# Opening of a two-layer decoder trunk: first weights from a second DMA queue in smaller pieces, and nine products of a cleared tile on TensorE ahead of the work

## Chip, cores and metric

One core of one Trainium2 chip. The time is device microseconds of one execution of the whole program; lower is better. All numbers of the trace are from one profiled execution of the kernel before.

## What is computed

The reference is a trunk of two layers over 256 tokens of 1024 channels in float32. Each layer adds half a SwiGLU, then a mixer (an S5 state space in the first, sparse attention in the second), then half a SwiGLU again. The change lies ahead of the first SwiGLU:

```python
def _rmsnorm(x, g):
    y = x * lax.rsqrt(jnp.mean(x * x, axis=-1, keepdims=True) + RMS_EPS)
    return y * g

def _swiglu(x, w_in, w_out):          # w_in: 1024 x 5632, w_out: 2816 x 1024
    a, b = jnp.split(x @ w_in, 2, axis=-1)
    return (jax.nn.silu(a) * b) @ w_out

h = h + 0.5 * _swiglu(_rmsnorm(h, ffn1_norm[0]), ffn1_w_in[0], ffn1_w_out[0])
```

## The kernel before

The 256 tokens are two token tiles of 128 rows, `h[:, 0]` and `h[:, 1]`. To multiply, the kernel needs h transposed: `Acts.fill(t, kq)` (L152) turns four 128 x 128 blocks on TensorE (L156) into a PSUM bank `tr` and splits them into a high and a low part, `xT`: ScalarE writes the rounded high part (L140), VectorE the difference (L141). Weights come in granules of 1 MB, `raw`, [128, 2048], that is four slabs of 512 columns; `rawp` holds two. `split_half` (L78) makes a high part `whi` (ScalarE, L96 with the gain of the norm, L86 without) and a low part `wlo` (VectorE, L99 or L92), for which there are five buffers of two slabs each. Every product is three matmuls (`mm3`, L112): high by high (L115), high by low (L116), low by high (L117).

The feed-forward block (`ffn`, L177) goes over 11 chunks c of 256 hidden channels. A chunk takes eight slabs of w_in (two granules) into two PSUM banks `mm`, one for each token tile; ScalarE and VectorE make g = silu(a) * b from them (L235, L236), which frees the banks. In the next chunk TensorE turns g (L190), ScalarE and VectorE split it into `gT` (L140, L141), and `second` (L200) multiplies it by one granule of w_out into four banks `o`, 24 matmuls. Chunk 0 takes token tile 0 first in groups of four slabs (`gemm`, `lead=True`), so that it can begin before tile 1 is there.

A granule's DMA is issued on SP (`load_granule`, L68) and waits until VectorE has done the last split of the granule that had the buffer. In the first block `background` queues steps of `s5_prepare` (L251) between the slabs: small VectorE operations on [128, 32] (names s_...), products on GpSimd and VectorE for the tables Cw, cosT, sinT. Each engine works its instructions strictly in the order that the scheduler of the framework has written; that order follows from the code and from the scheduler's own estimate of times.

The opening (L53 to L76) issues, all on SP: the identity, tile 0 of x, the gains, the first half of the first granule (`raw0`), tile 1 of x, the second half of `raw0`. Meanwhile ScalarE loads its table (L59). The next granules and the constants of S5 follow on SP.

Of the kernel before, what the change touches and what calls it, by code (L numbers as in the profile page):

```python
# [9 lines left out]
F32 = mybir.dt.float32  # L10
# [6 lines left out]
P = 128  # L17
# [15 lines left out]
def kernel(ctx: ExitStack, tc: tile.TileContext, A, out):  # L33
# [19 lines left out]
    # ---- constants and gains  # L53
# [3 lines left out]
    nhalf = pers.tile([P, 8], F32, name="nhalf")  # L57
    V.memset(nhalf, -0.5)
    S.activation(small.tile([P, 8], F32, name="warm"), nhalf, AF.Silu)  # L59
    nc.sync.dma_start(out=ident, in_=A["ident"])  # L60
    nc.sync.dma_start(out=h[:, 0, :], in_=A["x"][0])
    nc.sync.dma_start(out=gains, in_=A["gains"])

    # ---- weights: each granule is split exactly into hi + lo parts as it arrives, scaled by the gain of its rows
# [8 lines left out]
    raw0 = rawp.tile([P, 2048], F32, name="raw")  # L73
    nc.sync.dma_start(out=raw0[:, 0:1024], in_=A["w_in1_0"][0, 0][:, 0:1024])
# [3 lines left out]
    def split_half(raw, j, w, gain, k0, eng="av"):  # L78
        """eng: which engines round and subtract"""
# [39 lines left out]
    def gemm(acc, xT, gen, kts=KT, lead=False):  # L119
        """acc[t] = x[t] @ W over kts slabs; lead: token tile 0 goes first in groups of four slabs"""  # L120
# [8 lines left out]
    # ---- 1/rms of the rows of one token tile of h, from its two halves  # L129
# [14 lines left out]
    # ---- h^T as hi and lo parts, channels on partitions, with 1/rms of its rows  # L144
# [21 lines left out]
    def background(bg, n):  # L166
        """n steps of other work, queued behind what has been issued so far"""
# [8 lines left out]
    # ---- res += 1/2 SwiGLU(rmsnorm(h)); done(t, half) once a half of token tile t of res is complete  # L176
    def ffn(x, gi, w_in, w_out, res, perm=False, bg=None, steps=1, done=None, first=()):  # L177
        with tc.tile_pool(name="ffn", bufs=2) as fp, tc.tile_pool(name="ps_a", bufs=1, space=PSUM) as pa:
# [5 lines left out]
            def transposed(g):  # L184
                """g^T of one chunk, hi and lo, tokens in natural order"""
# [58 lines left out]
    # ---- S5 in chunks of four tokens: discretisation, rotation tables, and stationary operands  # L244
# [6 lines left out]
    def s5_prepare(kp, sp, W):  # L251
# [36 lines left out]
        def exp_parts(x):  # L288
            """2^n and exp(r) - 1 with x = n ln2 + r."""
# [53 lines left out]
        def products(x, y, t4_):  # L343
            """x_re y_re, x_im y_im, x_re y_im, x_im y_re"""
            for t_, i, j in zip(t4_, (0, 1, 0, 1), (0, 1, 1, 0)):
                tt(t_, x[i], b16(y[j]), ALU.mult, G)
# [118 lines left out]
    # ---- h += S5(rmsnorm(h)); token 4 c + 2 t + e is in row 64 e + c of token tile t  # L465
# [21 lines left out]
    def s5(hc, x, W, kp, done):  # L487
        cosT, sinT, Cw, Wi, WBT, r4 = W.cosT, W.sinT, W.Cw, W.Wi, W.WBT, W.r4
        with tc.tile_pool(name="s5r", bufs=1) as rp, tc.tile_pool(name="s5w", bufs=2) as wp, \
# [16 lines left out]
            def u_transposed(b0, nb):  # L506
                """u^T of 2 nb groups of 32 channels"""
# [13 lines left out]
            def rotated(cb):  # L521
                """the tables of four groups, for the real and the imaginary half"""
# [104 lines left out]
    # ---- shared keys and values  # L627
# [489 lines left out]
```

## Time and profile before

| | us |
|---|---|
| median of three runs | 1074.84 |
| lowest and highest run | 1074.09, 1077.22 |
| span of the profiled execution, first to last instruction | 1070.4 |
| TensorE busy in that span | 1002.3 |
| VectorE busy | 708.6 |
| ScalarE busy | 574.7 |

The profile shows the span, and the profiled execution has no other time of its own; the median of the runs is 4.4 us above it, which is what lies around the span. Matmuls are pipelined and their ends are modelled, so that the lengths of two neighbours overlap; the distance of their starts is what one of them costs. In a row of the timeline stand the start, the length, the engine, the line, the operation with out<-in, the shapes, and in brackets the idle time of the engine just ahead with what ended it. Names are those of the program without buffer numbers.

### The profile page before, as it was taken

What the parts mean: (1) busy time and instruction counts of PE and PEld (TensorE: products, weight loads), DVE (VectorE), ACT (ScalarE), POOL (GpSimd) and SP (SyncE); (2) the same over time, 40 slices, a digit from 0 to 9 for tenths busy, and PEclk for the clock granted to TensorE, in tenths of its full rate; (3) what the DMA queues carried; (4) which work ended last, traced back from release to release, by engine and by line L of the source; (5) the groups of instructions that cost most, each with busy time, mean ns of one, the idle gap of its engine ahead of it and who ended that gap; (6) DMA issues with size and microseconds to landing.
All of it is one profiled execution on the core that took longest, in us unless ns stands there. A gap on an engine that the chain in (4) does not pass through costs nothing.

```text
span 1070.4 us, 14818 instructions
## 1 busy us (share of the span) xinstructions
PE 1002.3 (94%) x5553; PEld 807.9 (75%) x5553; DVE 708.6 (66%) x1403; ACT 574.7 (54%) x1051; POOL 180.5 (17%) x185
## 2 busy tenths in 40 slices
PE   7978999988879899999999999999977899999998
PEld 6766877876657688887887888887866678888886
DVE  5999755949875465656757555655688866656553
ACT  6443566643335464655665555554786656545451
POOL 6375100305732000000005100000203220000000
PEclk9988999999989999999999999999988999999999
DMA  6553544420328865555464455554303146555551
GB/s 237 183 187 118 197 158 140 163 91 24 137 103 205 331 201 193 197 176 181 170 221 158 158 187 173 191 197 145 100 1 118 40 138 214 170 186 197 185 176 72
DMA packets 27912, 171.74 MB, mean 160 GB/s; under 512 B 4544, under 2 KB 4992, under 8 KB 9024
## 3 DMA queue, kind: packets, MB, share of 16 engines
q1 hardware_dynamic: 26192, 164.77, 44.5%
q0 software_dynamic: 1648, 6.03, 2.2%
q8 instruction: 43, 0.70, 0.3%
q14 instruction: 29, 0.24, 0.1%
HBM read 165.54 MB, written 5.24 MB: 160 GB/s over the span
## 4 chain that ended last, share of the span: by engine, by line
PE 73%; DVE 14%; DMA 4%; ACT 4%; POOL 3%; issue 2%; SPq 0%; ACTq 0%; POOLq 0%; DVEq 0%
PE mm L115 14%; PE mm L116 13%; PE mm L117 13%; PE o L117 7%; PE o L115 7%; PE o L116 7%; DMA raw<-in_w_in_dram 4%; DVE wlo L99 4%; DVE wlo L92 2%; PE tr L190 1%; DVE w L544 1%; ACT whi L96 1%; DVE Pt L906 1%; ACT Pt L895 1%; PE tr L913 1%
## 5 line engine op out<-in xcount | busy, mean ns | idle before, releaser
L99 DVE SCALAR_TENSOR_TENSOR wlo<-raw,gains,whi 128x512 fp32r<-128x512 f32 (+2 forms) x408 | 295.7, 759 | 130.6 <-ACT whi L96 126.7
L96 ACT ACTIVATE whi<-raw,gains 128x512 fp32r<-128x512 f32 (+2 forms) x408 | 267.3, 699 | 187.2 <-PE mm L117 60.8
L115 PE MATMUL mm<-whi,xT 128*128 128x512 f32 (+2 forms) x800 | 313.5, 392 | 4.5 <-ACT whi L96 3.5
L117 PE MATMUL mm<-whi,xT 128*128 128x512 f32 (+2 forms) x800 | 307.1, 384 | 0.0
L116 PE MATMUL mm<-wlo,xT 128*128 128x512 f32 (+2 forms) x800 | 306.8, 384 | 0.3 <-DVE wlo L99 0.3
L92 DVE TENSOR_TENSOR wlo<-raw,whi 128x512 fp32r<-128x512 f32 x192 | 135.0, 743 | 95.3 <-ACT whi L86 95.1
L86 ACT ACTIVATE whi<-raw 128x1024 fp32r<-128x1024 f32 x104 | 108.8, 1057 | 133.6 <-PE mm L117 62.1
L115 PEld LDWEIGHTS mm<-whi,xT 128*128 128x128 f32 x800 | 151.1, 189 | 36.0 <-ACT whi L96 4.8
L117 PEld LDWEIGHTS mm<-whi,xT 128*128 128x128 f32 x800 | 150.9, 189 | 29.8
L116 PEld LDWEIGHTS mm<-wlo,xT 128*128 128x128 f32 x800 | 151.2, 189 | 28.4 <-DVE wlo L99 1.1
L115 PE MATMUL o<-whi,gT 128*128 128x512 f32 x352 | 143.0, 406 | 9.5 <-ACT gT L140 9.5
L117 PE MATMUL o<-whi,gT 128*128 128x512 f32 x352 | 141.6, 404 | 8.1 <-DVE gT L141 7.9
L116 PE MATMUL o<-wlo,gT 128*128 128x512 f32 x352 | 141.4, 402 | 0.0
L115 PEld LDWEIGHTS o<-whi,gT 128*128 128x128 f32 x352 | 67.7, 192 | 27.5 <-ACT gT L140 11.9
L117 PEld LDWEIGHTS o<-whi,gT 128*128 128x128 f32 x352 | 67.6, 192 | 26.3 <-DVE gT L141 10.1
L116 PEld LDWEIGHTS o<-wlo,gT 128*128 128x128 f32 x352 | 67.7, 192 | 15.7
L235 ACT ACTIVATE g<-mm,rs 128x256 f32<-128x256 f32 x88 | 40.7, 471 | 27.7 <-PE mm L117 27.6
L236 DVE SCALAR_TENSOR_TENSOR g<-mm,rs,g 128x256 f32<-128x256 f32 x88 | 41.9, 483 | 19.9 <-ACT g L235 19.4
L141 DVE TENSOR_TENSOR gT<-tr,gT 128x512 fp32r<-128x512 f32 (+1 forms) x55 | 36.4, 661 | 25.9 <-ACT gT L140 25.6
L140 ACT ACTIVATE gT<-tr 128x512 fp32r<-128x512 f32 (+1 forms) x55 | 33.3, 605 | 33.4 <-PE tr L190 26.7
L137 POOL TENSOR_TENSOR rs<-ms,nhalf 128x1 f32<-128x1 f32 x12 | 7.2, 600 | 231.7 <-DVE ms L136 231.6
L895 ACT ACTIVATE Pt<-Pt,mx 128x128 f32<-128x128 f32 (+1 forms) x64 | 28.4, 445 | 6.4 <-DVE mx L890 6.3
(311 smaller groups left out, 1009.1 us busy)
## 6 DMA issues: line engine op xcount, KB each, us to landing
raw<-in_w_in_dram SPq DMA_DIRECT2D x87, 1024.0 KB, 4.9
raw<-in_w_out_dram SPq DMA_DIRECT2D x44, 1024.0 KB, 4.9
raw<-in_w_kv_dram SPq DMA_DIRECT2D x6, 1024.0 KB, 4.8
raw<-in_w_glu_dram SPq DMA_DIRECT2D x4, 1024.0 KB, 4.8
raw<-in_w_o_dram SPq DMA_DIRECT2D x4, 1024.0 KB, 4.9
revd<-rev POOLq DMA_DIRECT2D x8, 384.0 KB, 15.0
raw<-in_w_qg_dram SPq DMA_DIRECT2D x6, 512.0 KB, 3.6
B<-revd POOLq DMA_DIRECT2D x1, 2048.0 KB, 13.2
```

The source lines that it names most:

```text
L86: Last.act = S.activation(hi, r, AF.Copy)
L92: i = el.tensor_tensor(out=lo[:, c], in0=r[:, c], in1=hi[:, c].bitcast(F32), op=ALU.subtract)
L96: Last.act = S.activation(hi[:, c], r[:, c], AF.Identity, scale=g_)
L99: i = V.scalar_tensor_tensor(out=lo[:, c], in0=r[:, c], scalar=g_, in1=hi[:, c].bitcast(F32), op0=ALU.mult, op1=ALU.subtract)
L115: T.matmul(ps, lhsT=xh, rhs=wh, start=start, stop=False)
L116: T.matmul(ps, lhsT=xh, rhs=wl, start=False, stop=False)
L117: Last.pe = T.matmul(ps, lhsT=xl, rhs=wh, start=False, stop=stop_)
L140: i = S.activation(dst_hi, src, AF.Copy)
L141: V.tensor_tensor(out=dst_lo, in0=src, in1=dst_hi.bitcast(F32), op=ALU.subtract)
L235: Last.act = S.activation(sl, acc[t][:, 0:256], AF.Silu, scale=rs[:, t:t + 1])
L236: Last.dve = V.scalar_tensor_tensor(out=g[:, t, :], in0=acc[t][:, 256:512], scalar=rs[:, t:t + 1], in1=sl, op0=ALU.mult, op1=ALU.mult)
L895: S.activation(Pt[:, r, br], Pt[:, r, br], AF.Exp, scale=-1.0, bias=mx[:, c:c + 1], accum_out=sm[:, c:c + 1])
```

## The change

It does four things. The first half of `raw0` is issued on ScalarE's DMA queue in two pieces of 256 KB, ahead of ScalarE's table load. Tile 0 of x is issued on SP in two halves, and the identity and the gains come between them instead of ahead of the whole and behind it. VectorE clears a tile `blank` of 128 x 128, and TensorE multiplies it by itself nine times into a `tr` bank that nothing reads. Since these calls shift the estimate of the scheduler, it writes a different order on all engines for the first five chunks of the first feed-forward block; behind them the orders are the same.

```diff
+    raw0 = rawp.tile([P, 2048], F32, name="raw")
+    nc.scalar.dma_start(out=raw0[:, 0:512], in_=A["w_in1_0"][0, 0][:, 0:512])
+    nc.scalar.dma_start(out=raw0[:, 512:1024], in_=A["w_in1_0"][0, 0][:, 512:1024])
+    blank = small.tile([P, P], F32, name="blank", bufs=1)
+    V.memset(blank, 0.0)
     V.memset(nhalf, -0.5)
+    for i in range(2):
+        nc.sync.dma_start(out=h[:, 0, i * 512:(i + 1) * 512], in_=A["x"][0][:, i * 512:(i + 1) * 512])
+        if i == 0:
+            nc.sync.dma_start(out=ident, in_=A["ident"])
+            nc.sync.dma_start(out=gains, in_=A["gains"])
     S.activation(small.tile([P, 8], F32, name="warm"), nhalf, AF.Silu)
-    nc.sync.dma_start(out=ident, in_=A["ident"])
-    nc.sync.dma_start(out=h[:, 0, :], in_=A["x"][0])
-    nc.sync.dma_start(out=gains, in_=A["gains"])
...
-    raw0 = rawp.tile([P, 2048], F32, name="raw")
-    nc.sync.dma_start(out=raw0[:, 0:1024], in_=A["w_in1_0"][0, 0][:, 0:1024])
     nc.sync.dma_start(out=h[:, 1, :], in_=A["x"][1])
     nc.sync.dma_start(out=raw0[:, 1024:2048], in_=A["w_in1_0"][0, 0][:, 1024:2048])
...
                 x = Acts(h)
+                run = tr_bank()
+                for _ in range(9):
+                    T.matmul(run[:, 0:P], lhsT=blank, rhs=blank, start=True, stop=True)
                 for t in range(2):
                     for hf in range(2):
                         x.fill(t, hf)
```

In the changed file the same lines stand five further down (L96 is L101, L99 is L104, L140 and L141 are L145 and L146, L236 is L241, L260 is L265).

First place: ScalarE at the start of the program. xT is the high part of the transposed tiles, whi that of a slab, junk the squares for the norm. Before:

```order
L59 ACT_TABLE_LOAD
L59 ACTIVATE warm<-nhalf 128x8
L140 ACTIVATE xT<-tr 128x4x128
L96 ACTIVATE whi<-raw,gains 128x512
L140 ACTIVATE xT<-tr 128x4x128
L96 ACTIVATE whi<-raw,gains 128x512
L140 ACTIVATE xT<-tr 128x4x128 x2
L132 ACTIVATE junk,ss<-h 128x512
L96 ACTIVATE whi<-raw,gains 128x512
```

And now:

```order
L59 DMA raw<-in_w_in_0_dram 128x512
L60 DMA raw<-in_w_in_0_dram 128x512
L69 ACT_TABLE_LOAD
L69 ACTIVATE warm<-nhalf 128x8
L101 ACTIVATE whi<-raw,gains 128x512 x2
L145 ACTIVATE xT<-tr 128x4x128 x3
L101 ACTIVATE whi<-raw,gains 128x512
L145 ACTIVATE xT<-tr 128x4x128
L137 ACTIVATE junk,ss<-h 128x512
```

Two DMA issues have come to the front, and both splits of the first half granule now stand ahead of tile 0's xT. A little further on, chunk 1's first four splits stand ahead of chunk 0's g, where it was two before.

Second place: VectorE at the last four splits of chunk 2 (the granule ahead of which s_tr and behind which the w_out granule stands). s_... are the small operations of the S5 preparation; s_l1i and s_en are among those that GpSimd waits for. Before:

```order
L260 TENSOR_TENSOR s_tr<-s_et,s_t 128x32
L265 TENSOR_SCALAR s_t_364<-s_tr 128x32
L99 SCALAR_TENSOR_TENSOR wlo<-raw,gains,whi 128x512
L271 SCALAR_TENSOR_TENSOR s_cm_360<-s_t 128x32
L260 TENSOR_TENSOR s_l1i<-s_mag,s_sn 128x32
L265 TENSOR_SCALAR s_en<-s_cm_360 128x32
L99 SCALAR_TENSOR_TENSOR wlo<-raw,gains,whi 128x512
L260 TENSOR_TENSOR s_t<-s_em,s_en 128x32
L260 TENSOR_TENSOR s_l1r<-s_mag,s_en 128x32
```

And now:

```order
L104 SCALAR_TENSOR_TENSOR wlo<-raw,gains,whi 128x512
L265 TENSOR_TENSOR r_98<-s_t 128x32
L270 TENSOR_SCALAR s_et<-s_t 128x32
L104 SCALAR_TENSOR_TENSOR wlo<-raw,gains,whi 128x512
L272 TENSOR_SCALAR s_t<-s_et 128x32
L265 TENSOR_TENSOR s_tr<-s_et,s_t 128x32
L104 SCALAR_TENSOR_TENSOR wlo<-raw,gains,whi 128x512
L270 TENSOR_SCALAR s_t_378<-s_tr 128x32
L104 SCALAR_TENSOR_TENSOR wlo<-raw,gains,whi 128x512
L276 SCALAR_TENSOR_TENSOR s_cm_374<-s_t 128x32
L265 TENSOR_TENSOR s_l1i<-s_mag,s_sn 128x32
L270 TENSOR_SCALAR s_en<-s_cm_374 128x32
```

All four splits now stand ahead of s_l1i and s_en; before, the second came just behind s_en, the third five and the fourth thirteen small operations later. Behind this place chunk 1's gT has moved back by two splits and one Cw product, and chunk 2's by one split and one Cw product.

Third place: VectorE around chunk 3's gT (the last TENSOR_TENSOR with gT ahead of the end of the difference). Before:

```order
L99 SCALAR_TENSOR_TENSOR wlo<-raw,gains,whi 128x512 x2
L141 TENSOR_TENSOR gT<-tr,gT 128x512
L260 TENSOR_TENSOR sinT<-hy 128x512 x2
L99 SCALAR_TENSOR_TENSOR wlo<-raw,gains,whi 128x512 x2
L236 SCALAR_TENSOR_TENSOR g<-mm,rs,g 128x256 x2
L260 TENSOR_TENSOR sinT<-hy 128x512 x2
```

And now:

```order
L104 SCALAR_TENSOR_TENSOR wlo<-raw,gains,whi 128x512 x2
L265 TENSOR_TENSOR sinT<-hy 128x512
L146 TENSOR_TENSOR gT<-tr,gT 128x512
L265 TENSOR_TENSOR sinT<-hy 128x512
L104 SCALAR_TENSOR_TENSOR wlo<-raw,gains,whi 128x512 x2
L265 TENSOR_TENSOR sinT<-hy 128x512
L241 SCALAR_TENSOR_TENSOR g<-mm,rs,g 128x256
L265 TENSOR_TENSOR sinT<-hy 128x512
L241 SCALAR_TENSOR_TENSOR g<-mm,rs,g 128x256
```

One sinT product has moved ahead of gT, and chunk 4's two g products have moved behind the third and the fourth sinT product.

## The prediction

> **What bounds the kernel now.** I read the slices of the page first, then a table of stages, then the rows of TensorE that carry a wait.
>
> ```profile
> PE   7978999988879899999999999999977899999998
> DVE  5999755949875465656757555655688866656553
> ```
>
> Each digit covers 26.8 us. TensorE is not full in slice 1 (the opening) and in slices 3 and 4; there VectorE stands at 9. The first four slices are the first feed-forward block, which carries the S5 preparation on VectorE and GpSimd beside it. The next table gives busy time per stage (PE, PEld, DVE, ACT, POOL, then the granted clock).
>
> ```profile
> core 0: us, PE busy (x) PEld busy (x) DVE busy (x) ACT busy (x) POOL busy (x), PEclk, DMA share, GB/s
> 27.00:54.00 27.00, 25.09 (x114) 20.25 (x112) 25.52 (x78) 11.21 (x19) 10.14 (x15) 1.00 0.53 186
> 54.00:80.00 26.00, 20.25 (x79) 16.11 (x80) 24.56 (x27) 11.77 (x20) 20.64 (x17) 0.89 0.55 185
> 80.00:107.00 27.00, 22.18 (x86) 17.42 (x85) 25.92 (x30) 10.06 (x18) 16.14 (x12) 0.88 0.34 117
> 107.00:134.00 27.00, 27.00 (x138) 21.91 (x137) 19.32 (x41) 15.30 (x31) 4.02 (x6) 0.97 0.57 195
> ```
>
> From 27 to 107 us VectorE is idle for about 4 of 80 us and TensorE for 12.5; after 107 TensorE is never idle. So VectorE's queue sets the time up to about 102 us and TensorE the time after it. The rows of TensorE where that shows:
>
> ```profile
> 56.71 0.50 PE L117 MATMUL o<-whi,gT 128*128 128x512 f32 x1 [4.61 <-DVE gT L141]
> 78.06 0.79 PE L115 MATMUL o<-whi,gT 128*128 128x512 f32 x1 [3.05 <-ACT gT L140]
> 102.20 0.79 PE L117 MATMUL o<-whi,gT 128*128 128x512 f32 x1 [3.29 <-DVE gT L141]
> ```
>
> Each time TensorE waits for gT (the transposed SwiGLU product), which stands in VectorE's queue behind weight splits and S5 work. The last wait ends at 102.20. **What the change is worth is by how much gT comes earlier there**; a microsecond won on TensorE at 10 us is lost again in the 4.61 us wait unless VectorE's queue has moved as well.
>
> The opening itself, from the chain of waits (start, length, what):
>
> ```profile
> 2.12 4.92 DMA raw<-in_w_in_dram
> ...
> 7.13 0.73 ACT whi L96
> ...
> 7.90 0.80 PE mm L115
> 8.70 0.79 PE mm L116
> 9.48 1.71 PE tr L156 x8
> ```
>
> The first split waits until the half granule has landed at 7.04; TensorE then does two products and turns the second token tile.
>
> **Term 1, the opening: +1.3 us (0 to 2.1).**
>
> ```profile
> gains<-in_gains_dram SPq DMA_DIRECT2D x1, 24.0 KB, 3.3
> DMA to landing us min/median/max: 3.6/4.8/6.0
> 10.37 0.60 ACT L140 ACTIVATE xT<-tr 128x512 fp32r<-128x512 f32 x1 [1.43 <-PE tr L156]
> 16.02 1.94 ACT L96 ACTIVATE whi<-raw,gains 128x512 fp32r<-128x512 f32 x3
> 16.76 2.78 DVE L99 SCALAR_TENSOR_TENSOR wlo<-raw,gains,whi 128x512 fp32r<-128x512 f32 x3 [0.41 <-ACT whi L96]
> 15.08 4.81 SPq L70 DMA_DIRECT2D raw<-in_w_in_dram  x2
> ```
>
> The second line is for the two tiles of x: 3.6 us after its issue at 1.18 for tile 0, 6.0 after 2.59 for tile 1, so 4.8 and 8.6. After the change the first quarter of the weights and the first half of tile 0 are issued together at about 0.74: as many bytes as tile 0 before, begun 0.44 earlier, so 4.3. The gains have the same 600 KB ahead or beside them and land at about 4.9, as before (1.65 + 3.3). The first split then starts at 5.0 instead of 7.13. But ScalarE does nothing useful with most of these 2.1 us: next it needs tile 1 turned. Tile 1 has the same 1.1 MB ahead of it, begun 0.44 earlier, so it lands at 8.2, and its transposes start at 8.4 (before: 9.28, quoted below). The first four take 1.05 us at half clock and about 0.55 at full; between the two, ScalarE's unbroken run from 10.37 to 17.96 (16.02 + 1.94) begins at 9.25, 1.1 us earlier, VectorE's third split behind it ends at 18.3, not 19.54, and the reload that waits for it (the second of the two issues in the SP row) goes out 1.2 us earlier, the one before it 1.6. The ends: 0, if tile 1 lands when it did; 2.1, if all of the first split's lead survives. I take 1.3, by the row of tile 1. Three things are hidden. The two DMA issues on ScalarE (0.4 us each, as on SP) lie ahead of its table load, where it idles. SP's issue of the second granule now waits for the first quarter to land (4.3, not 3.54), with the S5 loads queued behind it; the 1.5 MB ahead of it keep the DMA engines busy past 8 us. And ScalarE now does two splits before it empties tile 0's transposes, so TensorE's first product comes at about 7.4, not 7.90, little of the 2.1 us; it is the second tile that counts.
>
> There is a rule that speaks against more. The Trainium skill, DMA: Bandwidth & Descriptors, section Issuing engines are not separate DMA queues, says that DMAs from all issuers run on the same 16 engines and interleave, so that a second issuer only saves issue time. By that the term would be one or two issue slots, about 0.5 us by SP's 0.47 us spacing, and the sum 0.8 us less; the overlap of tile 1's bytes above already follows it.
>
> **Term 2, waits of VectorE that go: +2.1 us (0 to 2.1).**
>
> ```profile
> 32.66 0.69 DVE L92 TENSOR_TENSOR wlo<-raw,whi 128x512 fp32r<-128x512 f32 x1 [0.67 <-ACT whi L86]
> 42.00 0.75 DVE L99 SCALAR_TENSOR_TENSOR wlo<-raw,gains,whi 128x512 fp32r<-128x512 f32 x1 [0.19 <-ACT whi L96]
> 69.91 4.68 DVE L92 TENSOR_TENSOR wlo<-raw,whi 128x512 fp32r<-128x512 f32 x4 [0.60 <-ACT whi L86]
> 78.04 0.69 DVE L141 TENSOR_TENSOR gT<-tr,gT 128x512 fp32r<-128x512 f32 x1 [0.66 <-ACT gT L140]
> 50.10 4.24 SPq L70 DMA_DIRECT2D raw<-in_w_in_dram  x2
> 54.92 1.33 ACT L96 ACTIVATE whi<-raw,gains 128x512 fp32r<-128x512 f32 x2 [6.81 <-DMA raw<-in_w_in_dram]
> ```
>
> 0.67 + 0.19 + 0.60 + 0.66 = 2.12. All four end on ScalarE, which had waited for a granule. A granule is issued when the last split of the buffer's former granule is done on VectorE (raw has two buffers). The new order puts splits ahead of S5 work and of g: chunk 1's third and fourth split now precede g, and chunk 2's last four stand together (front, second place). So the reload of 25.23 goes out at about 21.7, and the one of 50.10 at about 42.5 (start 39.2, four splits at 0.75 less overlap, five small operations); granules then lie ready when VectorE comes to them. What hides the longer TensorE stop behind g is the same 4.61 us wait. Low end 0: the waits come back elsewhere, for VectorE is the full engine.
>
> **Term 3, the shared time of GpSimd: +0.85 us (-0.85 to 0.85).**
>
> ```profile
> POOL cosT L260 <- DVE s_en L265: 24.1, 1, 24.1
> 46.77 1.60 DVE L99 SCALAR_TENSOR_TENSOR wlo<-raw,gains,whi 128x512 fp32r<-128x512 f32 x1
> 49.28 0.79 DVE L99 SCALAR_TENSOR_TENSOR wlo<-raw,gains,whi 128x512 fp32r<-128x512 f32 x1
> ```
>
> GpSimd starts its table products on a small VectorE result (s_en); while they run, the same split takes 1.60 instead of 0.75. In the new order all four splits of that granule precede s_en, which takes one such stretch out. If it falls on another operation, nothing is gained; on a longer one, as much is lost. The row is nearest to the gain.
>
> **Term 4, order ahead of the last gT: -0.68 us.** One of the two sinT products now stands in front of it (front, third place):
>
> ```profile
> 102.07 0.68 DVE L260 TENSOR_TENSOR sinT<-hy 128x512 f32<-128x512 f32 x1
> ```
>
> Chunk 4's two g products stand behind the last sinT products as well, which wait for GpSimd (front, third place). That is hidden as long as TensorE's 24 products behind the stop run at half clock, as now (102.20 to 110.2, 8 us); at full clock, 5.5 us, it would cost up to 2.
>
> **The blank products.**
>
> ```profile
> L596 PE MATMUL ga<-ident x20: 275/275/377, 233.7 to 235.9; 128*128 128x128 f32 x20
> 9.28 1.91 PE L156 MATMUL tr<-ident,h 128*128 128x128 f32 x8
> 12.27 0.63 PE L117 MATMUL mm<-whi,xT 128*128 128x512 f32 x1
> 12.70 0.44 PE L115 MATMUL mm<-whi,xT 128*128 128x512 f32 x1
> 12.97 0.39 PE L116 MATMUL mm<-wlo,xT 128*128 128x512 f32 x1
> ```
>
> Ten such products in the code of L596 are 20 instructions, started 2.2 us apart over 19 gaps: 0.115 each at full clock. Transposes of that size stand (1.91 - 0.42)/7 = 0.21 apart at 9.28, where products are 0.43 apart (12.27 to 12.70), against 0.23 to 0.27 after 12.70: the clock is half until then. So the nine are 18 instructions of 0.21, 3.8 us, from about 1.2 to 5.0, and end when tile 0 lands: they cost about 0.1. They gain what is in term 1; the seven slow products of 512 columns before 12.70 (1.4 us) lie where ScalarE's splits are late anyway, so they count nothing.
>
> Sum: 1.3 + 2.1 + 0.85 - 0.68 = 3.6 us. The span goes from 1070.4 to 1066.8; the median of the runs, 1074.84, is 4.4 above that span, and with it the time is **1071.2**. Nothing behind 102 us is changed, and TensorE is full there, so the gain stays.
>
> **Rivals.**
> A, **the waits only move**: VectorE is busy 95 of 100 parts of 27 to 107 us; a wait that goes is filled by another (its 0.96 us for GpSimd at 92.2, or gT now behind two more splits). Then terms 2 and 3 are 0: 1.3 - 0.68 = 0.6, so 1074.2. For it: three engines chase one another there. Against: ScalarE's 6.81 us wait at 54.92 is plainly a late reload.
> B, **the change doesn't do what it says**: the clock stays at half until 12.7 or later.
>
> ```profile
> 56.70:60.36 3.66, 3.65 (x9) 2.83 (x10) 3.56 (x6) 2.79 (x5) 3.66 (x4) 0.56 0.43 175
> 102.20:108.30 6.10, 6.10 (x14) 4.78 (x15) 5.55 (x7) 1.93 (x5) 5.48 (x4) 0.50 0.52 176
> ```
>
> After two stops of this trace the full clock came back after 3.7 and after 6.1 us of work, so 3.8 us of blanks may be too few. Tile 1's transposes are then all slow: 0.4 of term 1 is gone, 1071.6. The Trainium skill, TensorE: Matmul & The Clock Gate, Part 1, says that a free-running window of about 3.4 us must be busy; by that a burst of 3.8 us hits a full one seldom, with the transposes behind it often, and the two rows agree with one and with two windows.
> C, **slower: the blanks last too long**. No row shows them at half clock. At the 0.43 us of a slow 512-column product each, 18 take 7.7 us, to 8.9. Tile 0's transposes, at 4.92 now, wait for that, everything behind them is 4.0 late, the waits of term 2 stay, and term 4 adds 0.7; term 3 gives back 0.85 at most: 1074.84 + 4.0 + 0.7 - 0.85 = 1078.7. It begins to cost above 0.206 us each (1.2 + 18 x 0.206 = 4.9) and passes 0.3% at about 0.4.
>
> **Chances.** Forecast 0.54, A 0.26, B 0.12, C 0.08. A measurement of this kernel can tell about 0.3%, 3.2 us, from no change; the forecast lies 0.4 beyond that line, B on it. Faster by more: most of the forecast and half of B, 0.56; within: A and the rest, 0.35; slower: C and a little of A, 0.09. The range: the gain is at most 2.1 + 2.1 + 0.85 without term 4, 5.1, so 1069.7, and the runs scatter by a few tenths more; above it takes in A and leaves C out: 1069.3 to 1075.2.
>
> **What would show it.** Term 1: the first split at about 5.0, tile 1's transposes at 8.4, reloads at 13.5 and 18.3. Term 2: reloads near 21.7 and 42.5, no VectorE wait at 32 and 70. Term 3: no split of 1.6 us there. Sum: the last long wait for gT ends at 98.6 instead of 102.20. Blanks: products 0.23 apart before 9 us. I am wrong if that last wait ends at or after 101.5, or if TensorE stops again behind it.

## The result, and the profile after

| | before | after |
|---|---|---|
| median of 22 runs each, us | 1075.54 | 1073.09 |
| lowest to highest run | 1072.27 to 1079.12 | 1068.59 to 1075.76 |
| ratio, 95% interval | | 0.9976 (0.9966 to 0.9986) |
| span of the profiled execution | 1070.4 | 1070.4 |

The change takes 2.6 us off (1.5 to 3.7). That is 0.24%, a little under the 0.3% named in the prediction. The forecast was 1071.2, that is 3.6 us below the median of the three runs it started from; a gain of 3.6 us lies just inside the interval.

The slices of the changed kernel's page:

```profile
PE   8987999988889899999999999999987899999998
DVE  5999756849974465656757465555678866656553
```

The shape is that of before: VectorE full in slices 2 to 4, TensorE short of 9 in slices 1, 3 and 4. The table of stages to 107 us (PE, PEld, DVE, ACT, POOL busy, granted clock):

```profile
27.00:54.00 27.00, 25.73 (x116) 20.56 (x115) 26.39 (x83) 14.64 (x24) 9.21 (x13) 1.00 0.48 167
54.00:80.00 26.00, 23.19 (x96) 18.53 (x95) 25.75 (x30) 11.39 (x18) 20.51 (x19) 0.93 0.51 178
80.00:107.00 27.00, 20.85 (x79) 15.73 (x78) 26.05 (x28) 8.59 (x17) 18.84 (x14) 0.87 0.41 137
```

VectorE's busy time from 27 to 107 us went from 76.00 to 78.19 of 80 us: its waits have shrunk. Now the rows of the timeline that answer to those of before:

```profile
57.40 0.67 PE L122 MATMUL o<-whi,gT 128*128 128x512 f32 x1 [2.81 <-DVE gT L146]
100.16 0.79 PE L122 MATMUL o<-whi,gT 128*128 128x512 f32 x1 [3.85 <-DVE gT L146]
44.12 8.72 SPq L77 DMA_DIRECT2D raw<-in_w_in_dram  x2
89.57 2.14 DVE L265 TENSOR_TENSOR cosT<-hy 128x512 f32<-128x512 f32 x2 [0.95 <-POOL hy L265]
98.83 0.68 DVE L265 TENSOR_TENSOR sinT<-hy 128x512 f32<-128x512 f32 x1
99.43 0.68 DVE L146 TENSOR_TENSOR gT<-tr,gT 128x512 fp32r<-128x512 f32 x1
```

The stop at 56.71 is 1.8 us shorter, the one at 78.06 is gone, and the last one ends at 100.16 instead of 102.20. The reload of 50.10 goes out at 44.12. Between 26 and 112 us VectorE has one wait above 0.1 us left, the 0.95 us for GpSimd. The last two rows are term 4: gT now stands behind one sinT. Just ahead of that stretch a new wait has appeared:

```profile
25.48 0.75 DVE L104 SCALAR_TENSOR_TENSOR wlo<-raw,gains,whi 128x512 fp32r<-128x512 f32 x1 [1.40 <-ACT whi L101]
```

ScalarE waits there for the second granule of chunk 1 to land. In exchange a wait of 0.61 us for g, at 23.09 before, is gone.

The opening did not come earlier. First pieces from the head of the changed kernel's chain of waits, then rows of its timeline:

```profile
1.65 5.00 DMA gains<-in_gains_dram
...
6.74 1.34 ACT whi L101 x2
8.08 0.49 ACT xT L145
...
8.61 0.80 PE mm L120
```

```profile
1.06 4.21 PE L1008 MATMUL tr<-blank 128*128 128x128 f32 x18 [1.06 <-DVE nhalf L63]
5.91 1.09 PE L161 MATMUL tr<-ident,h 128*128 128x128 f32 x4 [0.65 <-DMA ident<-in_ident_dram]
9.63 1.05 PE L161 MATMUL tr<-ident,h 128*128 128x128 f32 x4
12.62 0.63 PE L122 MATMUL mm<-whi,xT 128*128 128x512 f32 x1
13.04 0.70 PE L120 MATMUL mm<-whi,xT 128*128 128x512 f32 x2
14.63 5.57 SPq L77 DMA_DIRECT2D raw<-in_w_in_dram  x2
```

The gains land at 6.65 us (4.9 was forecast), so the first split starts at 6.74, not 5.0; ScalarE empties tile 0's transposes only behind its two splits, at 8.08. The identity lands late too, tile 0 is turned at 5.91 (4.92 before), and TensorE's first product comes at 8.61, 0.7 us later than before. Products are at half clock until 13.04, where they were until 12.70. The first reload is 0.45 us earlier, but the second issue of that row is 0.3 us later (19.88 against 19.57), and the third pair of reloads (29.70 against 29.45) has nothing left of the lead.

So 2.0 us are won at the last wait for gT. At the same gT on VectorE more than 100 us later, before and then after:

```profile
226.44 0.69 DVE L141 TENSOR_TENSOR gT<-tr,gT 128x512 fp32r<-128x512 f32 x1 [5.67 <-ACT gT L140]
```

```profile
224.03 0.69 DVE L146 TENSOR_TENSOR gT<-tr,gT 128x512 fp32r<-128x512 f32 x1 [5.39 <-ACT gT L145]
```

The lead is 2.41 us. Yet both spans are 1070.4. The stretch behind, before and then after (the clock is the figure behind POOL's):

```profile
240.00:260.00 20.00, 15.79 (x303) 13.15 (x302) 18.79 (x48) 8.20 (x16) 9.20 (x11) 1.00 0.01 2
```

```profile
240.00:260.00 20.00, 19.03 (x305) 16.69 (x304) 17.47 (x43) 7.28 (x14) 9.82 (x12) 0.83 0.01 2
```

In this execution of the changed kernel TensorE runs part of the S5 stage at a lower clock (0.83 here), where the one of before did not (1.00). The change is not what decides that: over the fourteen kernels profiled for this document, the clock of this window is 1.00 in four (before, ab_only, dma_alone and best, explained below) and 0.69 to 0.83 in the others, with old and new orders in both groups.

Nor does a span of 1070.4 stand for the kernel before. Where a run has both on record, its time lies 1.7 to 2.1 us above its span, in one run 3.0, and not 4.4; the 4.4 us between the median and the span are not only what lies around the span. So the profiled execution of before took about 1072.2 us, an estimate from 1070.4 and the usual 1.8, which is one of its fastest. The median span is 1071.05 in the 22 runs of the changed kernel and 1074.4 to 1074.9 in three later series of runs of the one before. The forecast, a difference taken off a median, does not suffer from this; the equal spans are the chance of two executions.

### The profile page after: what moved, and what is told of

Same layout as the page of the kernel before. It is cut to its first block, busy times and chain, and to the rows that moved or that the text cites. A ratio compares the mean times of both kernels' runs of the same rounds, so it can differ in the third digit from the quotient of the medians.

```text
span 1070.4 us, 14864 instructions
## 1 busy us (share of the span) xinstructions
PE 1011.6 (95%) x5571; PEld 815.2 (76%) x5571; DVE 709.7 (66%) x1404; ACT 575.5 (54%) x1051; POOL 178.4 (17%) x185
## 4 chain that ended last, share of the span: by engine, by line
PE 70%; DVE 16%; DMA 5%; ACT 4%; POOL 3%; issue 2%; SPq 0%; ACTq 0%; POOLq 0%
PE mm L120 13%; PE mm L122 13%; PE mm L121 13%; PE o L122 7%; PE o L120 7%; PE o L121 7%; DVE wlo L104 4%; DMA raw<-in_w_in_dram 3%; DVE wlo L97 2%; PE tr L195 1%; DMA raw<-in_w_out_dram 1%; ACT whi L101 1%; DVE w L549 1%; DVE Pt L911 1%; POOL hrr L676 1%
## 5 line engine op out<-in xcount | busy, mean ns | idle before, releaser
L104 DVE SCALAR_TENSOR_TENSOR wlo<-raw,gains,whi 128x512 fp32r<-128x512 f32 (+2 forms) x408 | 297.2, 763 | 140.6 <-ACT whi L101 136.3
L101 ACT ACTIVATE whi<-raw,gains 128x512 fp32r<-128x512 f32 (+2 forms) x408 | 266.8, 698 | 192.0 <-PE mm L122 63.6
L241 DVE SCALAR_TENSOR_TENSOR g<-mm,rs,g 128x256 f32<-128x256 f32 x88 | 41.6, 481 | 18.5 <-ACT g L240 18.1
L146 DVE TENSOR_TENSOR gT<-tr,gT 128x512 fp32r<-128x512 f32 (+1 forms) x55 | 36.3, 660 | 24.6 <-ACT gT L145 24.2
L145 ACT ACTIVATE gT<-tr 128x512 fp32r<-128x512 f32 (+1 forms) x55 | 33.3, 606 | 32.9 <-PE tr L195 26.3
```

The source lines that it names most:

```text
L101: Last.act = S.activation(hi[:, c], r[:, c], AF.Identity, scale=g_)
L104: i = V.scalar_tensor_tensor(out=lo[:, c], in0=r[:, c], scalar=g_, in1=hi[:, c].bitcast(F32), op0=ALU.mult, op1=ALU.subtract)
L145: i = S.activation(dst_hi, src, AF.Copy)
L146: V.tensor_tensor(out=dst_lo, in0=src, in1=dst_hi.bitcast(F32), op=ALU.subtract)
L241: Last.dve = V.scalar_tensor_tensor(out=g[:, t, :], in0=acc[t][:, 256:512], scalar=rs[:, t:t + 1], in1=sl, op0=ALU.mult, op1=ALU.mult)
```

## Experiments

The question is which part of the change gives the 2.6 us. Theory O: the new order on VectorE and ScalarE. Theory P: the opening (transfers and blanks). One measure is used throughout, called **the ruler**: VectorE's queue from the third pair of w_in reloads on SP (29.45 us before, 29.70 after) to the pair at 113.88 (111.46). It leaves out the landing of the first transfers, which moves from one execution to the next: the third pair goes out at 29.1 to 31.5 us in the seven kernels with the transfers of before and at 29.4 to 30.7 in the five with those of the change and at most nine blanks. Its row, before and then after (the third busy time is VectorE's):

```profile
29.45:113.88 84.43, 71.95 (x294) 57.30 (x293) 79.39 (x137) 37.14 (x64) 50.71 (x47) 0.92 0.46 156
```

```profile
29.70:111.46 81.76, 71.53 (x296) 56.21 (x295) 79.85 (x139) 36.63 (x63) 50.68 (x47) 0.94 0.47 161
```

VectorE is busy for 79.4 and 79.9 us; idle for 84.43 - 79.39 = 5.04 and 81.76 - 79.85 = 1.91 us. The fourteen kernels on it ("last gT" is the end of TensorE's last long wait for gT, counted from the third pair):

| kernel | opening | order | ruler | busy | idle | last gT | ratio to before (95%) |
|---|---|---|---|---|---|---|---|
| before | before | before | 84.43 | 79.39 | 5.04 | 72.75 | 1 |
| blanks_alone | before + blanks | before | 84.59 | 80.12 | 4.47 | 72.89 | 1.000 (0.9984 to 1.0016) |
| old_order | after | before | 83.49 | 79.73 | 3.76 | 71.80 | 1.000 (0.9982 to 1.0017) |
| ab_only | before | chunks 0, 1 | 85.05 | 80.48 | 4.57 | 73.35 | 0.9991 (0.9971 to 1.0011) |
| c_only | before | chunk 2's splits | 84.84 | 79.66 | 5.18 | 73.15 | 0.9999 (0.9981 to 1.0017) |
| abc_only | before | both of these | 83.25 | 80.32 | 2.93 | 71.56 | 0.9988 (0.9968 to 1.0007) |
| abd_only | before | all but chunk 2's splits | 82.99 | 80.15 | 2.84 | 71.69 | 0.9983 (0.9971 to 0.9995) |
| after | after | after | 81.76 | 79.85 | 1.91 | 70.46 | 0.9976 (0.9966 to 0.9986) |
| order_only | before | after | 81.61 | 79.70 | 1.91 | 70.30 | 0.998 (0.9966 to 0.9995) |
| dma_alone | after, no blanks | after | 81.72 | 79.81 | 1.91 | 70.41 | 0.9971 (0.9955 to 0.9986) |
| gains_first | gains, identity first | after | 81.73 | 79.82 | 1.91 | 70.43 | 0.997 (0.9949 to 0.9991) |
| t4_back | after, no blanks | late gT and g as before | 82.17 | 79.30 | 2.87 | 70.47 | 0.9967 (0.9947 to 0.9988) |
| best | after, no blanks | late gT as before | 81.88 | 79.41 | 2.47 | 69.80 | 0.9971 (0.9958 to 0.9984) |
| blanks24 | after, 24 blanks | after | 81.57 | 79.66 | 1.91 | 70.26 | 0.9978 (0.9959 to 0.9996) |

Each row is one profiled execution. The three kernels with the order of before read 83.49 to 84.59, so differences of up to about 1 us are scatter; the five with the whole new order read 81.57 to 81.76.

How an order is kept: behind the last line of the program each named instruction is queued behind the one named ahead of it on its engine. That adds no wait between engines. The numbers are those of the instructions in the program before (a longer opening shifts them all alike; they are shown unshifted), in the first tuple VectorE's, in the second ScalarE's:

```diff
+    ORDER = (
+        (206, 210, 212, 292, 294, 369, 371, 239, 241, 254, 445, 256, 447,
...
+        (205, 209, 211, 291, 293, 368, 370, 238, 240, 444, 446, 474, 476,
...
+    )
+    traced = {i.name: i for i in nc.cur_bb.bb.instructions}
+    for names in ORDER:
+        for p, q in zip(names, names[1:]):
+            tc.add_manual_dep(traced[f"I-{q}"], f"I-{p}", mybir.DependencyInfo(mybir.DependencyClass.NoSync, mybir.DependencyReason.DATA), reason="order")
```

**order_only**: the diff above, on the kernel before.

> The kernel before, with its own transfers and no blank products; VectorE and ScalarE get the order of the changed kernel from behind the opening to the fifth chunk (151 and 37 instructions, by issue-order edges that add no wait). Theory O (the order is the gain): the reload of 50.10 us goes out near 44, VectorE's waits of 0.67 and 0.60 us at 32.66 and 69.91 are gone, the last long wait for gT ends at 100.2 +- 0.7 instead of 102.20, and the runs are 1.5 to 3.7 us faster than before. Theory P (the opening is the gain: transfers and blanks): the last wait ends at 102.2 +- 0.5 and the time is within 1 us of before.

```profile
9.05 0.72 ACT L96 ACTIVATE whi<-raw,gains 128x512 fp32r<-128x512 f32 x1 [2.18 <-DMA raw<-in_w_in_dram]
101.78 0.80 PE L117 MATMUL o<-whi,gT 128*128 128x512 f32 x1 [3.88 <-DVE gT L141]
```

In the profiled execution the first half granule landed 2 us later than in that of before (the first split waits until 9.05, not 7.13), and the last wait ends at 101.78, where P had it. Counted from the third pair, though, it ends 70.30 us behind, against 72.75 before and 70.46 after; VectorE's waits near 33 and 70 are gone (idle 1.91 us, as after), and the runs are 0.05 to 0.34% faster. That is O.

**old_order**: the changed kernel, with the same code and the order of before in the tuples (the order that the changed kernel has without it on the line with -):

```diff
-        (..., 292, 294, 369, 371, 239, 241, 254, 445, 256, 447, ...
+        (..., 292, 294, 239, 241, 254, 369, 256, 371, 258, 264, 445, ...
```

> The changed kernel with all its transfers and its nine blank products; VectorE and ScalarE get the order of before from behind the opening to the fifth chunk. Theory O: the reload goes out near 50 again, the last long wait for gT ends at 102.2 +- 0.7, and the time is within 1 us of before. Theory P: the last wait ends near 100.2 and the time is 1.5 to 3.7 us below before.

```profile
69.56 4.70 DVE L97 TENSOR_TENSOR wlo<-raw,whi 128x512 fp32r<-128x512 f32 x4 [0.62 <-ACT whi L91]
101.66 0.80 PE L122 MATMUL o<-whi,gT 128*128 128x512 f32 x1 [3.34 <-DVE gT L146]
```

With all transfers and blanks of the change, and the old order, the wait near 70 is back, the last wait ends at 101.66, and the ratio is 1.000. The opening alone gives nothing that can be measured, though the interval would still admit up to 1.9 us; the third pair, at 29.86, is not earlier than before (29.45) either.

**dma_alone**: the changed kernel without the blanks.

```diff
-    blank = small.tile([P, P], F32, name="blank", bufs=1)
-    V.memset(blank, 0.0)
...
-                run = tr_bank()
-                for _ in range(9):
-                    T.matmul(run[:, 0:P], lhsT=blank, rhs=blank, start=True, stop=True)
```

> The changed kernel without the blank tile and its nine products; the order of VectorE and ScalarE stays that of the changed kernel but for four instructions. Theory O: the last wait ends at 100.2 +- 0.7 and the runs are 1.5 to 3.7 us faster than before, as with the blanks. Theory P with the blanks as its cause: within 1 us of before. In both, tile 0 is turned within 0.3 us of 5.91, if the identity sets that and not the blanks, and the clock rises at the end of a stretch of 3.41 us of products, between 11 and 15 us.

```profile
5.43 1.09 PE L159 MATMUL tr<-ident,h 128*128 128x128 f32 x4 [5.43 <-DMA ident<-in_ident_dram]
10.20 0.57 PE L119 MATMUL mm<-wlo,xT 128*128 128x512 f32 x1
10.61 0.40 PE L120 MATMUL mm<-whi,xT 128*128 128x512 f32 x1
99.77 0.79 PE L120 MATMUL o<-whi,gT 128*128 128x512 f32 x1 [3.53 <-DVE gT L144]
```

The gain is whole without the blanks. Tile 0 waits for the identity (5.43, a little under the expected band). The clock is full from about 10.5 us, ahead of the band, and so in this execution earlier than with nine blanks in that of the changed kernel.

**blanks_alone**: the kernel before, with the lines that dma_alone takes out.

> The kernel before with the blank tile and its nine products ahead of tile 0; its transfers stay, and its order but for four places. Theory O: the blanks run from about 1.1 to 5.3 at 0.22 us an instruction, tile 0 is turned 0.4 us later than 4.92, the last long wait ends at 102.2 +- 0.7 and the time is within 1 us of before. Theory P with the blanks as its cause: products stand 0.23 us apart before 9.3 us, and the time is 1.5 us or more below before.

```profile
5.08 1.86 PE L158 MATMUL tr<-ident,h 128*128 128x128 f32 x8
8.24 0.49 PE L117 MATMUL mm<-whi,xT 128*128 128x512 f32 x1 [1.30 <-ACT whi L98]
9.37 1.16 PE L158 MATMUL tr<-ident,h 128*128 128x128 f32 x8
10.76 0.63 PE L117 MATMUL mm<-whi,xT 128*128 128x512 f32 x1
11.18 0.63 PE L118 MATMUL mm<-wlo,xT 128*128 128x512 f32 x1
```

Time and last wait (102.33) are those of before; tile 0 is turned 0.16 us later (0.4 expected). Eight transposes take 1.86 us at 5.08 and 1.16 at 9.37, and then products stand 0.42 apart again. So the clock did rise behind the blanks, and it was half again by 10.76, behind waits of 1.30 and 0.29 us. That these waits lost it is likely; no run takes them away. P is out with these four: the order alone gives the gain, and neither part of the opening gives one that shows.

Next, which places of the order. **ab_only** and **c_only** are order_only with the order of before in part of the tuples. In ab_only chunk 2's splits (584, 586, 610, 612) and all that follows are as before; in c_only these four alone are moved ahead of s_l1i (391) and s_en (363), with ScalarE's part of it. The diff is c_only against before:

```diff
-        ..., 365, 584, 361, 391, 363, 586, 386, 389, 394, 387, 396, 610, ...
+        ..., 584, 347, 351, 586, 353, 355, 610, 365, 612, 361, 391, 363, ...
```

> The kernel before, its own opening; only the first two changed places of the order (VectorE and ScalarE, chunks 0 and 1: four splits of chunk 1 ahead of chunk 0's g, w_out's four splits and two more ahead of chunk 1's gT and g) are those of the changed kernel. The ruler is VectorE's queue from the third pair of reloads (29.45 us before, 29.70 after) to the pair at 113.88 (111.46): 84.4 us before, 81.8 after. Theory C (the gain comes from chunk 2's four splits ahead of the S5 operations): at least 83.4 us here, the reload of 50.10 still after 48.5. Theory AB (it comes from the first two chunks): at most 82.4 us.

> The kernel before, its own opening; only the third changed place of the order (VectorE and ScalarE, chunk 2: its last four splits ahead of s_l1i and s_en) is that of the changed kernel. Theory C: the reload of 50.10 goes out near 45, the 0.6 us wait at 69.91 is gone, the ruler from the third pair of reloads to the pair at 113 reads at most 82.6 us, and the runs are 1.0 to 3.0 us faster than before. Theory AB: the reload is earlier too, but the ruler reads at least 83.4 us and the time is within 1 us of before.

First a row of ab_only, then two of c_only:

```profile
71.03 4.69 DVE L92 TENSOR_TENSOR wlo<-raw,whi 128x512 fp32r<-128x512 f32 x4 [1.58 <-ACT whi L86]
```

```profile
46.47 8.74 SPq L70 DMA_DIRECT2D raw<-in_w_in_dram  x2
43.12 0.75 DVE L99 SCALAR_TENSOR_TENSOR wlo<-raw,gains,whi 128x512 fp32r<-128x512 f32 x1 [1.06 <-ACT whi L96]
```

Both theories fall. ab_only loses the waits near 33 and 42 and gets them back at 71 (1.58 instead of 0.60). c_only sends the reload 15.9 us behind the third pair instead of 20.65, and the wait that grows is at 43 (1.06 instead of 0.19). Neither place by itself wins anything that the ruler (85.05 and 84.84) or the runs (ratios around 1) show. This is rival A of the prediction, in the small.

**abc_only** joins the two; **abd_only** is order_only with only chunk 2's splits as before:

```diff
-        ..., 584, 347, 351, 586, 353, 355, 610, 365, 612, 361, 391, 363, ...
+        ..., 347, 351, 353, 355, 365, 584, 361, 391, 363, 586, ..., 610, ..., 612, ...
```

> The kernel before, its own opening; the first three changed places of the order (chunks 0 to 2) together are those of the changed kernel, the later ones (chunk 1's gT and chunk 2's g behind chunk 3's splits, chunk 2's and 3's gT, chunk 4's g) stay as before. The ruler from the third pair of reloads to the pair at 113 has read VectorE's busy time of 80.3 to 81.6 us plus its waits in all ten kernels so far. Theory W (the wait near 70 belongs to the fourth place): it stays, 0.5 to 1.6 us, with 0.95 us twice for GpSimd, and the ruler reads 83.0 to 84.6 us. Theory K (the first three places together remove it): at most 82.4 us, and the time is 1.5 us or more below before.

> The kernel before, its own opening; the order of the changed kernel on VectorE and ScalarE, but for chunk 2's four splits, which stand among the S5 operations as before. Theory N (those four splits are needed: without them the reload of 50.10 us stays at 48 or later and chunk 3's splits, now ahead of chunk 1's gT, wait for it): VectorE waits 1 us or more between 50 and 72 and the ruler reads at least 83.0 us. Theory D (the later places do it alone): waits of at most 0.5 us there, the ruler reads at most 82.4 us, and the time is 1.5 us or more below before.

First a row of abc_only (the last sinT still waits for GpSimd), then three of abd_only:

```profile
107.46 0.69 DVE L260 TENSOR_TENSOR sinT<-hy 128x512 f32<-128x512 f32 x1 [0.95 <-POOL hy L260]
```

```profile
49.16 4.24 SPq L70 DMA_DIRECT2D raw<-in_w_in_dram  x2
68.35 1.29 DVE L92 TENSOR_TENSOR wlo<-raw,whi 128x512 fp32r<-128x512 f32 x2 [0.56 <-ACT whi L86]
69.95 3.09 DVE L92 TENSOR_TENSOR wlo<-raw,whi 128x512 fp32r<-128x512 f32 x2 [0.31 <-ACT whi L86]
```

Neither theory holds whole for abc_only: the wait near 70 is gone although W kept it, and the ruler of 83.25 is in W's band and above K's 82.4, because the 0.95 us for GpSimd remain and VectorE was busy 0.5 us longer than in the changed kernel. In abd_only the reload stays late and VectorE waits 0.87 us near 70, between the bounds of N and D. So of the three groups (chunks 0 and 1, chunk 2's splits, the later places) the two pairs that were tried read 1.2 and 1.4 us below before on the ruler, about half of the 2.7 us that all three give. How much each group is worth is not shown by that: the difference is hardly more than the scatter of one order, abd_only's ratio (0.9983) can't be told from the changed kernel's, and at the gT near 224 us it is as early (223.88 against 224.03). The later places by themselves, and with chunk 2's splits alone, were not tried.

**t4_back** is dma_alone with chunk 3's gT (882) ahead of both sinT (982, 983) and chunk 4's g (917, 919) together, as before; **best** moves the gT alone.

```diff
-        ..., 967, 969, 982, 882, 983, 991, 993, 1006, 917, 1007, 919, ...
+        ..., 967, 969, 882, 982, 983, 991, 993, 1006, 917, 1007, 919, ...
```

> The changed kernel without the blanks, and with chunk 3's gT and chunk 4's two g in the order of before (gT ahead of the first sinT, both g together behind the second split). By term 4 of the prediction the last long wait for gT ends 0.6 to 0.7 us earlier than without this edit (99.77), near 99.15, and VectorE waits 0.95 us for GpSimd ahead of the last sinT again; TensorE is full behind it, so the time is 0.3 to 0.7 us below the kernel without the blanks. Rival: the last wait moves but the 0.95 us come out behind it, and TensorE stops there or the pair at 111 goes out 0.3 us later or more.

> The changed kernel without the blanks; its order, with one instruction moved: chunk 3's gT stands ahead of the first sinT, as before the change, while chunk 4's two g stay behind and between the last sinT products, where they cover the 0.95 us wait for GpSimd. The ruler reads 81.6 to 81.8 us as without the edit, the last long wait for gT ends 0.6 us earlier counted from the third pair of reloads (69.8 us behind it instead of 70.4), and the runs are 0.3 to 0.8 us below those without the blanks, which the interval can't resolve. Rival: the half clock behind the stop hides the 0.6 us, and the time is that without the blanks.

A row of best:

```profile
106.92 0.69 DVE L263 TENSOR_TENSOR sinT<-hy 128x512 f32<-128x512 f32 x1 [0.56 <-POOL hy L263]
```

best has its last wait at 69.80 behind the third pair, 0.61 earlier than dma_alone, as term 4 says, but 0.56 us of waiting for GpSimd came out behind it. In t4_back the wait for GpSimd is 0.95 again (idle 2.87), and the 0.6 us did not show (70.47): between two reloads (45.18 and 63.30 us) VectorE, never idle there, took 1.8 us longer than in best for the same order, with longer operations beside GpSimd. On VectorE the g between the sinT products cover 0.95 us of GpSimd, and moving gT ahead takes part of that back (best's ruler of 81.88 is just above the expected band). In the runs neither differs from dma_alone, so the runs show no worth of either place, and they can't tell best's expectation from its rival.

**gains_first** is dma_alone, its order kept, with gains and identity at the head of SP's queue:

```diff
+    nc.sync.dma_start(out=gains, in_=A["gains"])
+    nc.sync.dma_start(out=ident, in_=A["ident"])
     for i in range(2):
         nc.sync.dma_start(out=h[:, 0, i * 512:(i + 1) * 512], in_=A["x"][0][:, i * 512:(i + 1) * 512])
-        if i == 0:
-            nc.sync.dma_start(out=ident, in_=A["ident"])
-            nc.sync.dma_start(out=gains, in_=A["gains"])
```

> The changed kernel without the blanks, its order kept from behind the opening, and on SP the gains and the identity ahead of tile 0's halves instead of behind the first. Theory G (the gains' landing holds the first split, and what the opening gains goes through): gains land at 3.5 us or before, the first split starts at 5.3 to 5.9, when the first quarter has landed, instead of 6.31, the first reload goes out 0.4 us or more before 14.31 and the last wait for gT ends 0.3 us or more before 99.77. Rival: tile 0, now behind the identity, or tile 1 sets the start; the first reload stays within 0.3 us of 14.31 and so does the last wait of 99.77.

```profile
4.41 0.72 ACT L98 ACTIVATE whi<-raw,gains 128x512 fp32r<-128x512 f32 x1 [1.25 <-DMA raw<-in_w_in_dram]
6.68 1.94 PE L158 MATMUL tr<-ident,h 128*128 128x128 f32 x8 [6.68 <-DMA h<-in_x_dram]
15.27 4.82 SPq L74 DMA_DIRECT2D raw<-in_w_in_dram  x2
```

The first split starts at 4.41, as early as the prediction wanted it and earlier than either theory here. It wins nothing: tile 0 now lands at 6.6 and the first reload is 1 us later than in dma_alone. Of the rival the mechanism holds, that tile 0 sets the start, but not its numbers: the first reload and the last wait (100.31) are 1.0 and 0.5 us later than in dma_alone, not within 0.3. What comes first on the queues here delays what comes next.

**blanks24**: `range(24)` for `range(9)`, order kept.

> The changed kernel with 24 blank products instead of nine (48 instructions), its order of VectorE and ScalarE kept from behind the opening. By windows of 3.41 us that must be full: the clock rises between 4.5 and 7.9 us, the blanks stand 0.21 us apart until then and 0.11 after, end between 8.4 and 9.8, and tile 0 is turned then instead of at 5.91; the clock stays full through tile 1, and the first reload goes out 0.3 to 2 us later than 14.63. If a delay of the opening goes through to the end, the last wait for gT ends as much later than 100.16, and the runs are 0.3 to 2 us above the changed kernel's. Rival: the full clock makes good for the wait, and the first reload is at 14.3 or earlier.

The rows are stretches with the blanks alone (TensorE's busy time and count):

```profile
1.06:6.90 5.84, 5.84 (x27) 5.84 (x28) 1.00 0.82 257
6.90:9.30 2.40, 2.40 (x23) 2.40 (x21) 1.00 1.05 434
```

```profile
12.80 5.98 SPq L77 DMA_DIRECT2D raw<-in_w_in_dram  x2
98.84 0.80 PE L122 MATMUL o<-whi,gT 128*128 128x512 f32 x1 [3.96 <-DVE gT L146]
```

A blank takes 5.84 / 27 = 0.22 us up to 6.9 and 2.40 / 23 = 0.10 after: the clock rises inside the burst, in the stretch that was expected (4.5 to 7.9), and both tiles are turned at full clock. Tile 0 is turned behind the burst, at 9.36, and the first reload goes out at 12.80, 1.8 us earlier than in the changed kernel (three splits of the weights also stand earlier in its opening, so the clock is not the only cause). So the rival holds, and so long a burst costs nothing that the runs show. Of the 1.8 us, 1.1 are left at the third pair (28.58), and the last wait ends 1.3 us earlier than in the changed kernel (98.84); the ratio of the runs does not show them, and its interval of 0.19% on either side is too wide to deny them.

## Why the prediction was right, and where not

VectorE's queue from the third pair to the start of its last gT (101.47 and 99.43), before and then after, splits the result by the terms:

```profile
29.45:101.47 72.02, 60.27 (x255) 47.96 (x253) 68.08 (x119) 31.24 (x50) 42.74 (x39) 0.95 0.46 156
```

```profile
29.70:99.43 69.73, 60.23 (x257) 47.13 (x255) 67.98 (x122) 30.58 (x49) 43.10 (x39) 0.97 0.47 161
```

| | forecast | measured | from |
|---|---|---|---|
| term 1, opening | +1.3 | -0.25 | third pair 29.45 to 29.70 |
| term 2, waits | +2.1 | +2.19 | idle 72.02 - 68.08 = 3.94 to 69.73 - 67.98 = 1.75 |
| term 3, shared time | +0.85 | +0.7 | busy 68.08 to 67.98, though one sinT of 0.60 is added |
| term 4, one sinT ahead | -0.68 | -0.60 | sinT 98.83, gT 99.43 |
| at the last wait for gT | 3.6 | 2.04 | 102.20 to 100.16 |

**What bounds it: right.** On the ruler VectorE's busy time is 79.3 to 80.5 us in all fourteen kernels; its idle time goes from 1.9 to 5.2, so what differs between them is above all its waiting.

**Term 1: wrong, the whole miss.** The 1.3 us stood on tile 1's transposes starting at 8.4. They started at 9.63, although tile 1 had landed at about 8.5 (issued at 2.59, 5.9 us to landing; 8.2 forecast): on TensorE they stand behind the first two products, which began at 8.61 and not at 7.4. The step that failed ahead of that is the sentence that the gains "have the same 600 KB ahead or beside them and land at about 4.9, as before (1.65 + 3.3)". The row says 1.65 + 5.00, and the chain of waits goes from there through the two splits and xT to the first product. The identity, for which the term has no price, landed a microsecond too late for tile 0 as well. gains_first shows that the gains were not the only cover: with the first split at 4.41, tile 0 was late instead. old_order measures the whole opening at 1.000. The working had a loose end of its own: the ScalarE run begins 1.1 us earlier, but the two reloads that hang on it are put at 1.2 and 1.6 without saying where the rest comes from. The Trainium skill, DMA: Bandwidth & Descriptors, section Issuing engines are not separate DMA queues, says that transfers from all issuers interleave on the same engines, so that a second issuer only saves issue time; the trace agrees, as nothing is left of the opening's lead at the third pair (29.70 against 29.45), and adds a price, below.

**Term 2: right on the ruler.** All four waits of the forecast went. Ahead of the third pair, which the table books under term 1, waits only changed place: 1.12 and 0.61 us before (at 20.66 and 23.09), 0.62 and 1.40 after (at 20.46 and 25.48). The reloads came at 23.23 and 44.12 us (21.7 and 42.5 forecast), 1.5 and 1.6 late, about what the opening failed to give. The experiments add what I did not see: the waits hang together, and the places that were tried singly won nothing that shows. The four waits are no proof of the new order one by one, though: blanks_alone and old_order keep the order of before and do not have those near 33 and 78 either. What sets the orders apart is the idle time of the whole ruler, 1.91 us in all five kernels with the new order and 3.76 to 5.04 in the three with the old.

**Term 3: near in size, but not shown.** The split of 1.60 us is gone, but the stretch fell on a fourth small operation instead: four of them take 1.05 to 1.10 us after (44.55 to 47.74), three take 1.05 before (43.64 to 45.79). The 0.7 us lie with the splits of the whole window: its 42 took 43.4 us before, 15 of them above 1.2 us each, and 41.3 after, with 12 such; small operations and Cw products took part of that back. No run singles out the order as the cause. VectorE's busy time on the ruler is 79.4 to 80.1 us in the three executions with the order of before and 79.7 to 79.9 in the five with the new one, so a gain of this kind can't be told from scatter; that the number came near is luck.

**Term 4: right** (0.61 in best). Its other half, chunk 4's g behind and between the last sinT products, was not just hidden: it covers the 0.95 us wait of 108.70, and VectorE is 2.42 us ahead behind it (111.46 against 113.88). That this reaches the end is not shown: t4_back, without it, is as fast in the runs (0.9967).

**Rivals.** A is wrong for the whole change and right for ab_only and c_only. B came true in the profiled execution: products stood 0.43 apart until 13.04. Whether it has a part in the miss stays open. blanks_alone had the clock up for a while and was no faster than before. blanks24, with full clock for both tiles, has its first reloads at 12.80 and 18.45 (13.5 and 18.3 forecast for the change) and its last wait at 98.84 (98.6 forecast), though its gains land late too; but it is one execution, three splits stand elsewhere in its opening, and its runs are no faster than the changed kernel's. C is wrong: a blank instruction takes 0.21 to 0.22 us, and even the 48 of blanks24 cost nothing that shows.

No version beat the changed kernel by more than the intervals. Without the second queue (order_only) and without the blanks (dma_alone) the gain is there all the same; what these runs show to be worth keeping is the order.

## What to carry to other kernels

Where one engine is full for a stretch, count its waits from a fixed event inside that stretch, not from the start: its busy time hardly changes, and the gain is the waiting that goes. Waits that follow from each other through buffers (a late split, a late reload, a late conversion) have to go together; one that went alone came back later in the stretch (ab_only, c_only). And when an edit shifts a scheduler's estimate, keep the old order under the new code, and the new order under the old code, before crediting the edit.

## What the hardware did that I had not expected

- Small transfers landed later in the openings with a second queue. The gains (24 KB) took 3.3 to 3.6 us from issue to landing in before, order_only, blanks_alone, ab_only and c_only, and 4.4 to 5.0 in after, old_order, dma_alone, t4_back, best and blanks24; the identity (64 KB) 1.8 to 1.9 and 4.0 to 4.6. The gains stand third on SP in both, with fewer bytes ahead of them on SP after the change; the identity moved from first to second. In gains_first, at the head of their queue, gains took 3.4 and the identity, behind it, 4.1. No run has the second queue as its only difference, so the cause is argued.
- The half clock ended for good at 12.70 us before, 10.5 in dma_alone and 11.8 in t4_back, all without blanks, and at 13.04 after, 11.7 in old_order and about 13.4 in blanks_alone, all with nine: the nine did not bring that forward. The Trainium skill, TensorE: Matmul & The Clock Gate, Part 1, says that one busy window of about 3.4 us lifts the clock and that the windows run freely; blanks24 agrees (lifted 5.9 us after its first blank, within two windows). In blanks_alone the lift was gone behind waits of 1.30 and 0.29 us; why so short waits went with it, no run here shows.
- VectorE beside GpSimd: an operation of 0.18 us can take 1.05, and which one does differs between executions of the same order. Between t4_back and best, in a stretch with the same order and no waiting, a reload moved by 1.8 us.
